# Seven Strassen quarter products for the eight of a down projection, in a one-layer streaming encoder step

## Chip, cores and metric

The kernel runs on one core of a Trainium2 chip, in one launch. The metric is the device time in microseconds (us). The kernel before took 2740.11 us as the median of three runs (2739.68, 2740.11 and 2749.0).

## The reference

One step of a one-layer encoder in float32, for 2048 prompt tokens and 64 sample tokens of width 1024. The mixer (a gated linear recurrence with four heads, and a gated recurrent unit with a short convolution) stands ahead of the part that changes; six modulation vectors come from a matrix `w_ada` for the prompt and for the sample each.

```python
mod = jax.nn.silu(c) @ w_ada + b_ada
sh1, sc1, g1, sh2, sc2, g2 = jnp.split(mod[:, None, :], N_MOD, axis=-1)
hn = _rms(x) * (1 + sc1) + sh1
...
x = x + g1 * y
hn2 = _rms(x) * (1 + sc2) + sh2
x = x + g2 * (jnp.square(jax.nn.relu(hn2 @ w_up)) @ w_down)
...
y = _rms(x) * final_gain
```

`w_up` is 1024 x 4096, `w_down` 4096 x 1024. The change is to the product with `w_down`.

## The kernel before, in words

The prompt is worked on in four blocks of 512 tokens; the last block carries the 64 sample tokens too. A block goes through phase A (first norm and its transpose, `XT`), the projections and mixers, phase O (output projection, residual, second norm), and the MLP. Every float32 product is made of three matmuls of split operands (`HL`): high by high, high by low, low by high. `split_raw` (L245) makes both parts of a weight unit of 128x1024: ScalarE casts the high part (L247), and VectorE or GpSimd subtracts it for the low part (L248). `CFG` says which engine: of the up units each second one went to GpSimd, the down units to VectorE.

The MLP goes over eight groups of 512 columns. `phase_U` (U) of a group is 96 matmuls of 128x512 (L901) into the PSUM pool `pmu`; ScalarE takes relu (L904) and its square as the high part (L906), VectorE squares again (L907) and subtracts for the low part (L908), into a tile `gt` of the pool `mgp` (two buffers). `phase_D` (D) is 96 matmuls (L942; 112 in the last block, with the sample) into `pmd`, two buffers, one PSUM tile for each 128 tokens and 512 output columns; VectorE adds each to its row of `acc` in SBUF (L946; ScalarE copies in the first group). The last group, D7, multiplies by the gate (L948), adds (L949) to what phase F0 has made of `acc` on GpSimd (L965, L966), and ends with the final norm (phase F).

The program writes U0, U1, D0, U2, D1 and so on, U7, phase A of the next block, D6, D7. `sec` gives each part a rank from which the scheduler makes the order of every engine's queue. SyncE issues all loads. Within blocks 0 to 2, from the second group on, some sums of the sample's modulation vectors stand between (`ada_s`, run 5 times a block): VectorE takes a loaded tile of `w_ada` times one entry of silu(c) for each partition and adds it up, in 256 columns at a time (`ada_first`, L271, L273) or 1024 (`ada_part`, L308, L310); one tiny matmul for each 128 columns (L280, L314) sums over partitions. These loads used the pool `vop`, five buffers.

## Time and profile before

| | us |
|---|---|
| median of three runs | 2740.11 |
| span of the profiled execution | 2745.4 |
| TensorE busy (L901 745.3, L942 754.2) | 2554.4 |
| VectorE busy | 1635.4 |
| ScalarE busy | 946.6 |
| GpSimd busy | 481.7 |
| weight splits L248 on VectorE (253) / GpSimd (131) | 314.9 / 319.1 |

The profiled execution's span is 5.3 us above the median of the runs. Its granted TensorE clock was 0.965 of the full 2.4 GHz over the span. Busy time is the time in which an engine has an instruction under way; an instruction that waits inside the engine for a port counts as busy, so an operation's duration can hold a wait. "Releaser" in a row, behind `<-`, is the instruction whose end let the next one start.

### The profile page before, as it was taken

Reading aid. Unit: us, or ns where it says so; the run is one execution under the profiler, and the core shown is the slowest. Engines: PE = TensorE matmul, PEld = TensorE weight load, DVE = VectorE, ACT = ScalarE, POOL = GpSimd, SP = SyncE. Lnnn points to the kernel's source line nnn. Section 1 sums busy time; section 2 is a strip of 40 time slices with the busy share of each in tenths; the row PEclk is TensorE's granted clock in tenths of the full one; section 3 lists DMA queues with packets and bytes.
Section 4 is the critical chain, followed back from the end, with each engine's and each line's share of the span. In section 5 each row is a group of like instructions: output and inputs, shape, how many; then the busy total and the mean of one; then the engine's idle time right before and its main releaser. Section 6 shows DMA issues by size and latency. Waiting matters only on the chain.

```text
span 2745.4 us, 35118 instructions
## 1 busy us (share of the span) xinstructions
PE 2554.4 (93%) x13868; PEld 2180.5 (79%) x13868; DVE 1635.4 (60%) x3007; ACT 946.6 (34%) x1511; POOL 481.7 (18%) x292
## 2 busy tenths in 40 slices
PE   5898999999988999999898999999898899999996
PEld 4876887887866788888776788888798788988995
DVE  6678745566466765554746874544736677344446
ACT  4353442223325353223325253222322625422321
POOL 2311111011322110100323111010323211011003
PEclk8998999999999999999999999999999999999998
DMA  6242434444411335444511233423432233222222
GB/s 235 93 158 80 169 130 139 142 149 161 138 47 62 115 110 168 135 135 145 175 55 62 85 126 113 153 89 104 158 108 62 32 101 109 92 81 77 88 89 74
DMA packets 93477, 311.75 MB, mean 114 GB/s; under 512 B 15072, under 2 KB 17024, under 8 KB 92288
## 3 DMA queue, kind: packets, MB, share of 16 engines
q1 hardware_dynamic: 93312, 309.50, 34.0%
q8 instruction: 109, 1.79, 0.3%
q14 instruction: 56, 0.46, 0.0%
HBM read 291.60 MB, written 17.86 MB: 113 GB/s over the span
## 4 chain that ended last, share of the span: by engine, by line
PE 73%; DVE 18%; issue 3%; ACT 3%; DMA 2%; POOL 1%; SPq 0%; DVEq 0%; ACTq 0%; POOLq 0%
PE ps_u L901 26%; PE ps_d L942 20%; PE ps_in L584 7%; PE ps_vo L695 6%; PE ps_y L867 4%; PE ps_lv L770 3%; DVE hd_h L774 2%; DVE rsp L350 1%; DVE wt L248 1%; PE ps_in L569 1%; DVE hd_h L775 1%; PE ps_rg L644 1%; DVE rgtmp L640 1%; DMA x_a<-in_x_prompt_dram 1%; DVE acc L949 1%
## 5 line engine op out<-in xcount | busy, mean ns | idle before, releaser
L942 PE MATMUL ps_d<-wt,gt 128*128 128x512 f32 x3200 | 754.2, 396 | 32.6 <-DVE hd_f L948 14.8
L901 PE MATMUL ps_u<-XT,wt 128*128 128x512 f32 (+2 forms) x4128 | 745.3, 341 | 13.7 <-DVE XT L377 9.2
L942 PEld LDWEIGHTS ps_d<-wt,gt 128*128 128x128 f32 x3200 | 605.4, 191 | 172.8 <-DVE acc L946 19.5
L901 PEld LDWEIGHTS ps_u<-XT,wt 128*128 128x128 f32 x4128 | 656.6, 190 | 95.1 <-DVE XT L377 10.8
L247 ACT CAST wt<-raw 128x1024 fp32r<-128x1024 f32 x384 | 400.0, 1046 | 500.8 <-PE ps_d L942 386.7
L248 POOL TENSOR_TENSOR wt<-raw,wt 128x1024 fp32r<-128x1024 f32 x131 | 319.1, 2443 | 1274.1 <-ACT wt L247 1253.9
L248 DVE TENSOR_TENSOR wt<-raw,wt 128x1024 fp32r<-128x1024 f32 x253 | 314.9, 1246 | 370.5 <-ACT wt L247 370.3
L584 PE MATMUL ps_in<-XT,wt 128*128 128x512 f32 (+1 forms) x1776 | 392.9, 370 | 7.0 <-POOL wt L248 3.9
L584 PEld LDWEIGHTS ps_in<-XT,wt 128*128 128x128 f32 x1776 | 296.7, 195 | 50.8 <-issue 5.0
L904 ACT ACTIVATE hd_u<-ps_u 128x512 f32<-128x512 f32 (+2 forms) x172 | 85.6, 498 | 463.0 <-PE ps_u L901 462.9
L946 DVE TENSOR_TENSOR acc<-acc,ps_d 128x512 f32<-128x512 f32 x204 | 138.7, 682 | 153.7 <-PE ps_d L942 153.6
L695 PE MATMUL ps_vo<-wt,XT 128*128 128x256 f32 x1600 | 205.6, 288 | 7.7 <-ACT vo L704 6.0
L695 PEld LDWEIGHTS ps_vo<-wt,XT 128*128 128x128 f32 x1600 | 199.4, 195 | 9.9 <-ACT vo L704 5.9
L907 DVE TENSOR_TENSOR hd_u<-hd_u 128x512 f32<-128x512 f32 (+2 forms) x172 | 148.3, 862 | 97.9 <-ACT gt L906 97.8
L867 PE MATMUL ps_y<-wt,mix 128*128 128x512 f32 x800 | 195.7, 399 | 0.6 <-DVE rst L346 0.3
L867 PEld LDWEIGHTS ps_y<-wt,mix 128*128 128x128 f32 x800 | 149.1, 190 | 32.5 <-DVE rst L346 0.7
L770 PEld LDWEIGHTS ps_lv<-hd_h 128*128 128x128 f32 x640 | 92.8, 218 | 48.8 <-issue 33.7
L770 PE MATMUL ps_lv<-hd_h 128*128 128x64 f32 x640 | 95.3, 298 | 36.2 <-DVE hd_h L775 35.0
L774 DVE TENSOR_TENSOR hd_h<-hd_h 128x256 f32<-128x256 f32 x112 | 79.8, 712 | 51.5 <-PE ps_lv L770 40.4
L310 DVE SCALAR_TENSOR_TENSOR ada_acc<-raw,silc,ada_acc 128x1024 f32<-128x1024 f32 x56 | 76.3, 1363 | 39.9 <-DMA raw<-in_w_ada_dram 39.5
L908 DVE TENSOR_TENSOR gt<-hd_u,gt 128x512 fp32r<-128x512 f32 (+2 forms) x172 | 97.0, 564 | 4.7
L906 ACT ACTIVATE gt<-hd_u 128x512 fp32r<-128x512 f32 (+2 forms) x172 | 91.3, 533 | 1.3
(261 smaller groups left out, 1981.6 us busy)
## 6 DMA issues: line engine op xcount, KB each, us to landing
raw<-in_w_up_dram SPq DMA_DIRECT2D x128, 512.0 KB, 3.6
raw<-in_w_down_dram SPq DMA_DIRECT2D x128, 512.0 KB, 3.5
raw<-in_w_in_dram SPq DMA_DIRECT2D x96, 512.0 KB, 3.5
raw<-in_w_ada_dram SPq DMA_DIRECT2D x80, 512.0 KB, 3.6
raw<-in_w_out_dram SPq DMA_DIRECT2D x32, 512.0 KB, 3.5
x_a<-in_x_prompt_dram SPq DMA_DIRECT2D x16, 512.0 KB, 4.5
x<-in_x_prompt_dram SPq DMA_DIRECT2D x16, 512.0 KB, 5.2
x2d<-x SPq DMA_DIRECT2D x16, 512.0 KB, 3.0
```

The source lines that it names most:

```text
L247: S.copy(wt[:, 0], raw)
L248: eng.tensor_tensor(wt[:, 1], raw, wt[:, 0].bitcast(F32), op=ALU.subtract)
L584: T.matmul(ps[:, :pn], lhsT=w[:, a, k], rhs=B.XT.p[x][:, k, p0:p0 + pn], start=(k == 0 and q == 0), stop=(k == KD - 1 and q == 2))
L695: T.matmul(ps[:rows(B.toks[ti]), :256], lhsT=l, rhs=ws[k // 4][:, a, k % 4], start=(q == 0), stop=(q == len(ops) - 1))
L770: T.matmul(ps[:C, c * C // 2:(c + 1) * C // 2].rearrange("p (b h) -> p b h", h=hs), lhsT=KS[:, c * C:c * C + C], rhs=qv[:, c * bc:(c + 1) ...
L774: V.tensor_tensor(qv[:, :, 1], qv[:, :, 1], tv[:, :, 0:1].to_broadcast([P, nb, hs]), op=ALU.mult)
L867: T.matmul(ps[:rows(B.toks[ti])], lhsT=l, rhs=ws[k - k % 2][:, a, k % 2], start=(q == 0), stop=(q == len(ops) - 1))
L901: T.matmul(ps[:, :pn], lhsT=w[:, a, k], rhs=B.XT.p[x][:, k, p0:p0 + pn], start=(k == 0 and q == 0), stop=(k == KD - 1 and q == 2))
L907: V.tensor_mul(r, r, r)
L908: B.ulast = V.tensor_tensor(gt.p[1][:, c, p0:p0 + pn], r, gh.bitcast(F32), op=ALU.subtract)
L942: T.matmul(ps[:nr], lhsT=l, rhs=ws[half][c // 2][:, a, c % 2], start=(q == 0), stop=(q == len(ops) - 1))
L946: V.tensor_tensor(ac[:nr, sl], ac[:nr, sl], ps[:nr], op=ALU.add)
```

## The change

Of the eight groups' D, the first seven become W (`phase_W`): the product of the group's activations (512 tokens x 512) with its weights (512 x 1024) is cut into quarters and formed from seven products of quarters in place of eight (Strassen's scheme in Winograd's form). A product is two token tiles of six matmuls: 84 for a W, where D had 96; the sample's tokens get 16 of their own as before. The products M1, M6 and M7 are accumulated over the seven groups in tiles of their own (`accM`), the others in the quarters of `acc`; `combine` adds them up once a block, ahead of D7. `down_units` makes the seven weight operands, `sums_of` the seven of the activations, in two tiles `gX` and `gY` that take both buffers of `mgp`. The product order is A11, A12, S1, S4, S2, S3, A22, their PSUM tiles by turns in `pmd` (two buffers) and `pax` (three).

```diff
-CFG = dict(hd=2, w=6, raw=3, gr='G', f0='GGGGG', blk=32, proj='GG', proj0='GV', vo0='GG', vo='VV', up='VG', down='VV')
+CFG = dict(hd=2, w=5, raw=5, gr='G', f0='GGGGG', blk=32, proj='GG', proj0='GV', vo0='GG', vo='VV', up='VV', down='VV')
...
-    vop = pool("vop", 5)
+    vop = pool("vop", 7)
...
+    def ada_raw(src):
+
+        raw = rowp.tile([P, 1028], F32, tag="row", name="raw")[:, :1024]
...
+        def split(n, raw):
+            hi, lo = op[n]
+            S.copy(hi, raw)
+            return V.tensor_tensor(lo, raw, hi.bitcast(F32), op=ALU.subtract)
+
+        split("A11", A11)
+        split("A12", A12)
+        split("A22", A22)
+        V.tensor_tensor(A22, A21, A22, op=ALU.add)
+        split("S1", A22)
+        V.tensor_tensor(A21, A11, A21, op=ALU.subtract)
+        V.tensor_tensor(A11, A22, A11, op=ALU.subtract)
+        V.tensor_tensor(A12, A12, A11, op=ALU.subtract)
+        split("S4", A12)
+        split("S2", A11)
+        B.ulast = split("S3", A21)
...
+    def down_units(g):
...
+        w11, w21 = split(r11), split(r21)
+        E.tensor_tensor(r11, r12, r11, op=ALU.subtract)
+        t1 = split(r11)
+        w22 = split(r22)
+        E.tensor_tensor(r11, r22, r11, op=ALU.subtract)
+        t2 = split(r11)
+        E.tensor_tensor(r12, r22, r12, op=ALU.subtract)
+        t3 = split(r12)
+        E.tensor_tensor(r21, r21, r11, op=ALU.subtract)
+        t4 = split(r21)
...
+        M1, M6, M7 = (B.accM[n] for n in (1, 6, 7))
+        lo, hi = slice(0, 512), slice(512, 1024)
+        for t in range(2):
+            add(G, B.acc[t][:, lo], M1[:, t])
+        add(V, M6, M1)
+        for t in range(2):
+            add(V, B.acc[t][:, hi], M6[:, t])
+        for t in range(2):
+            add(V, B.acc[t][:, hi], B.acc[2 + t][:, hi])
+        add(G, M7, M6)
+        for t in range(2):
+            av = B.acc[2 + t].rearrange("p (h c) -> p h c", h=2)
+            add(G, av, M7[:, t].unsqueeze(1).to_broadcast([P, 2, 512]))
...
+            if g:
+                with sec(b, 115 + 10 * g):
+                    (phase_D if g == NG else phase_W)(B, g - 1, gts[g - 1])
             if g == NG - 1 and not B.last:
                 with sec(b, 182):
                     phase_A(blocks[b + 1], B.ulast)
             if g:
-                with sec(b, 115 + 10 * g):
-                    phase_D(B, g - 1, gts[g - 1])
```

`E` in `down_units` is GpSimd; VectorE's own square is left out for the first seven groups, and `hd` goes from ScalarE's square straight to `sums_of`. The up splits all go to VectorE. The loads of `w_ada` for the sample go through `rowp`, two buffers. The gate matrices `rgw` and the sample's state are loaded once a block into `vop`, the gate matrices laid out on the host; the sample's low parts are no longer copied a second time for `gt` and `mix`. The last line of the diff writes the next block's phase A behind W6 instead of ahead of D6; it is still gated on U7's last split.

The order of the engines' queues moves in three places.

**First place.** VectorE in the MLP of block 0, where the sample's first modulation vectors are summed. Before (L271, L273, L277: the modulation sums; L907, L908: U's square and low part; L946: the evacuation):

```order
L907 TENSOR_TENSOR hd_u<-hd_u 128x512
L273 SCALAR_TENSOR_TENSOR ada_acc<-raw,silc,ada_acc 128x256
L908 TENSOR_TENSOR gt<-hd_u,gt 128x512
L273 SCALAR_TENSOR_TENSOR ada_acc<-raw,silc,ada_acc 128x256 x3
L277 TENSOR_TENSOR ada_acc<-ada_acc 128x256
L907 TENSOR_TENSOR hd_u<-hd_u 128x512
L946 TENSOR_TENSOR acc<-acc,ps_d 128x512
L908 TENSOR_TENSOR gt<-hd_u,gt 128x512
L271 TENSOR_SCALAR ada_acc<-raw,silc 128x256
L273 SCALAR_TENSOR_TENSOR ada_acc<-raw,silc,ada_acc 128x256
L946 TENSOR_TENSOR acc<-acc,ps_d 128x512 x2
```

Now (L268, L270, L282: the same sums; L938: the split of an activation operand; L1042: the evacuation of W):

```order
L938 TENSOR_TENSOR gX<-hd_u,gX 128x512
L286 TENSOR_TENSOR modc<-ps_ada,cols 128x2
L270 SCALAR_TENSOR_TENSOR ada_acc<-raw,silc,ada_acc 128x256 x2
L282 TENSOR_TENSOR ada_acc<-ada_acc 128x256
L268 TENSOR_SCALAR ada_acc<-raw,silc 128x256 x2
L270 SCALAR_TENSOR_TENSOR ada_acc<-raw,silc,ada_acc 128x256 x6
L282 TENSOR_TENSOR ada_acc<-ada_acc 128x256
L268 TENSOR_SCALAR ada_acc<-raw,silc 128x256
L270 SCALAR_TENSOR_TENSOR ada_acc<-raw,silc,ada_acc 128x256 x3
L1042 TENSOR_TENSOR accM<-accM,ps_d 128x512 x2
L1042 TENSOR_TENSOR acc<-acc,ps_d 128x512 x4
```

The sums stood between squares and evacuations; now they stand in one block behind the last split of the activation sums and ahead of the group's first evacuation.

**Second place.** GpSimd over one group of block 0. Before, the 16 operations of the eight groups' up units stood in one row, two of them a group:

```order
L248 TENSOR_TENSOR wt<-raw,wt 128x1024 x16
```

Now one group is (L1011: the split of a weight operand; L1015, L1020, L1018, L1022: the weight sums):

```order
L1015 TENSOR_TENSOR raw<-raw 128x1024
L1020 TENSOR_TENSOR raw<-raw 128x1024
L1011 TENSOR_TENSOR wt<-raw,wt 128x1024 x2
L1018 TENSOR_TENSOR raw<-raw 128x1024
L1022 TENSOR_TENSOR raw<-raw 128x1024
L1011 TENSOR_TENSOR wt<-raw,wt 128x1024 x5
```

Eleven operations of 128x1024 stand where two stood (the last of the five splits in the bottom row is the first of the next group).

**Third place.** VectorE behind the fourth product's evacuation of W6, at the end of a block (L1071: the combination; L245: weight splits of D7 and, the last, of the next block; L1111: D7's first results; L489: the next block's norm):

```order
L1042 TENSOR_TENSOR accM<-accM,ps_d 128x512 x4
L1042 TENSOR_TENSOR acc<-acc,ps_d 128x512
L1071 TENSOR_TENSOR accM<-accM 128x1024
L1042 TENSOR_TENSOR acc<-acc,ps_d 128x512
L1071 TENSOR_TENSOR acc<-acc,accM 128x512 x2
L1071 TENSOR_TENSOR acc<-acc 128x512 x2
L245 TENSOR_TENSOR wt<-raw,wt 128x1024 x3
L1111 TENSOR_TENSOR hd_f<-ps_d,row 128x512
L245 TENSOR_TENSOR wt<-raw,wt 128x1024
L489 TENSOR_SCALAR ss_a<-ss_a 128x4
```

and GpSimd in the same place (L1128, L1129: phase F0):

```order
L1011 TENSOR_TENSOR wt<-raw,wt 128x1024 x3
L1071 TENSOR_TENSOR acc<-acc,accM 128x512 x2
L1011 TENSOR_TENSOR wt<-raw,wt 128x1024
L1071 TENSOR_TENSOR accM<-accM 128x1024
L1071 TENSOR_TENSOR acc<-acc,accM 128x1024 x2
L1128 TENSOR_TENSOR acc<-acc,row 128x1024 x4
L1129 TENSOR_TENSOR acc<-acc,x2r 128x1024 x4
```

Ten operations of the combination have come in ahead of D7 and of phase F0; three weight splits of D7 stand behind VectorE's part of them.

## Rows read from the trace of the kernel before

**Rows 1.** The page's head and part 1: busy time, share, count by engine.

```profile
span 2745.4 us, 35118 instructions
...
PE 2554.4 (93%) x13868; PEld 2180.5 (79%) x13868; DVE 1635.4 (60%) x3007; ACT 946.6 (34%) x1511; POOL 481.7 (18%) x292
```

**Rows 2.** The page, part 4: the chain that ended last, by engine.

```profile
PE 73%; DVE 18%; issue 3%; ACT 3%; DMA 2%; POOL 1%; SPq 0%; DVEq 0%; ACTq 0%; POOLq 0%
```

**Rows 3.** Windows (busy PE, PEld, DVE, ACT, POOL; PEclk; DMA): with, without modulation work.

```profile
1083.11:1128.44 45.33, 45.33 (x210) 37.66 (x208) 21.67 (x26) 13.51 (x17) 4.79 (x2) 1.00 0.33 105
1816.94:1860.81 43.87, 43.87 (x196) 36.06 (x195) 18.09 (x24) 11.41 (x15) 4.98 (x3) 1.00 0.30 96
```

**Rows 4.** Timeline of TensorE: one U, the D behind it (block 1).

```profile
1037.52 21.92 PE L901 MATMUL ps_u<-XT,wt 128*128 128x512 f32 x96
1059.28 5.60 PE L942 MATMUL ps_d<-wt,gt 128*128 128x512 f32 x24
```

**Rows 5.** The page, part 5: the weight split on GpSimd and VectorE.

```profile
L248 POOL TENSOR_TENSOR wt<-raw,wt 128x1024 fp32r<-128x1024 f32 x131 | 319.1, 2443 | 1274.1 <-ACT wt L247 1253.9
L248 DVE TENSOR_TENSOR wt<-raw,wt 128x1024 fp32r<-128x1024 f32 x253 | 314.9, 1246 | 370.5 <-ACT wt L247 370.3
```

**Rows 6.** By line (ns min/median/max): modulation step L310, evacuation L946.

```profile
L310 DVE SCALAR_TENSOR_TENSOR ada_acc<-raw,silc,ada_acc x56: 1271/1284/2558, 130.1 to 1763.2; 128x1024 f32<-128x1024 f32 x56
...
L946 DVE TENSOR_TENSOR acc<-acc,ps_d x204: 671/680/689, 423.5 to 2693.4; 128x512 f32<-128x512 f32 x102
```

**Rows 7.** Timeline of VectorE, 1100 to 1116 us (block 1).

```profile
1102.34 0.68 DVE L907 TENSOR_TENSOR hd_u<-hd_u 128x512 f32<-128x512 f32 x1
1103.06 0.69 DVE L908 TENSOR_TENSOR gt<-hd_u,gt 128x512 fp32r<-128x512 f32 x1
1107.16 2.46 DVE L907 TENSOR_TENSOR hd_u<-hd_u 128x512 f32<-128x512 f32 x1 [3.42 <-ACT gt L906]
```

**Rows 8.** Timeline of GpSimd, the same stretch.

```profile
1106.68 2.40 POOL L248 TENSOR_TENSOR wt<-raw,wt 128x1024 fp32r<-128x1024 f32 x1 [30.88 <-ACT wt L247]
```

**Rows 9.** Timeline of GpSimd, 609 to 616 us (block 0).

```profile
611.30 3.16 POOL L248 TENSOR_TENSOR wt<-raw,wt 128x1024 fp32r<-128x1024 f32 x1 [8.19 <-ACT wt L247]
```

**Rows 10.** Timeline of VectorE, the same stretch.

```profile
610.20 0.35 DVE L271 TENSOR_SCALAR ada_acc<-raw,silc 128x256 f32<-128x256 f32 x1 [2.13 <-DMA raw<-in_w_ada_dram]
610.59 0.49 DVE L273 SCALAR_TENSOR_TENSOR ada_acc<-raw,silc,ada_acc 128x256 f32<-128x256 f32 x1
610.99 1.22 DVE L248 TENSOR_TENSOR wt<-raw,wt 128x1024 fp32r<-128x1024 f32 x1
```

**Rows 11.** Timeline of GpSimd, phase F0 at the end of block 3.

```profile
2703.07 5.59 POOL L965 TENSOR_TENSOR acc<-acc,row 128x1024 f32<-128x1024 f32 x2 [11.90 <-DVE rsq L351]
2708.63 4.71 POOL L966 TENSOR_TENSOR acc<-acc,x2r 128x1024 f32<-128x1024 f32 x2
```

**Rows 12.** Timeline of VectorE, the same stretch.

```profile
2711.03 5.63 DVE L949 TENSOR_TENSOR acc<-acc,hd_f 128x512 f32<-128x512 f32 x2 [3.39 <-POOL acc L966]
...
2719.58 2.14 DVE L949 TENSOR_TENSOR acc<-acc,hd_f 128x512 f32<-128x512 f32 x1
```

**Rows 13.** The page, part 6: modulation loads, last column issue to landing.

```profile
raw<-in_w_ada_dram SPq DMA_DIRECT2D x80, 512.0 KB, 3.6
```

**Rows 14.** Windows: boundary behind block 0, a stretch inside it.

```profile
643.82:704.68 60.86, 52.35 (x222) 42.32 (x220) 44.99 (x70) 22.62 (x39) 19.85 (x8) 0.92 0.49 175
...
666.00:672.00 6.00, 5.01 (x16) 4.36 (x17) 3.56 (x10) 1.68 (x3) 2.36 (x1) 0.50 0.17 66
```

**Rows 15.** Timeline of TensorE at that boundary.

```profile
666.99 2.05 PE L470 MATMUL ps_rs<-ident,rsq 128*128 128x128 f32 x8 [3.77 <-DVE rsq L351]
...
693.58 4.42 PE L942 MATMUL ps_d<-wt,gt 128*128 128x512 f32 x12 [2.99 <-DVE hd_f L948]
```

**Rows 16.** Tile x_a: loads; VectorE timeline: last write of XT.

```profile
L449 SPq DMA_DIRECT2D x_a<-in_x_prompt_dram x12: 327/328/579, 648.6 to 1943.2; - x12
...
685.33 0.73 DVE L481 SCALAR_TENSOR_TENSOR XT<-x_a,modc,XT 128x512 fp32r<-128x512 f32 x1
```

More of the change, by code (lines that the diff above doesn't have):

```diff
@@ L97, in layout @@
     xt = a["x_prompt"][0].reshape(-1, BLK, 4, 2, P)
+    gate_w = np.zeros((P, 4, 2, P), np.float32)
+    for m, nm in enumerate(("rg_wa", "rg_wx")):
+        for c in range(4):
+            for hf in range(2):
+                sl = slice(hf * 64, hf * 64 + 64)
+                gate_w[sl, c, m, sl] = a[nm][0][2 * c + hf]
+    d["rg_w"] = gate_w.reshape(P, D)
     d["x_t"] = np.ascontiguousarray(xt.transpose(0, 2, 4, 3, 1)).reshape(-1, 4, P, 2 * BLK)
@@ L811, in hg_chunks @@
             if g.which:
-                dst = Sst_s[:, h]
+                dst = B.Ss[:, h]
             else:
@@ L904, in phase_U @@
             S.activation(r, ps[:, :pn], AF.Relu)
+            if not plain:
+                S.activation(r, r, AF.Square)
+                continue
             gh = gt.p[0][:, c, p0:p0 + pn]
@@ new lines, in phase_W, with evac @@
+    def phase_W(B, g, op):
+        if g == 0:
+            B.acc = [vop.tile([P, D], F32, tag="vo", name="acc") for _ in range(4)]
+            B.accM = {n: vop.tile([P, 2, 512], F32, tag="vo", name="accM") for n in (1, 6, 7)}
+            if B.last:
+                B.acc.append(adp.tile([P, D], F32, tag="ada", name="acc_s"))
+        ws = down_units(g)
+        M = {n: [B.accM[n][:, t] for t in range(2)] for n in (1, 6, 7)}
+        for n, ti, half in ((2, 0, 0), (3, 0, 1), (4, 2, 0), (5, 2, 1)):
+            M[n] = [B.acc[ti + t][:, half * 512:half * 512 + 512] for t in range(2)]
+        def evac(dst, ps):
+            if g == 0:
+                return S.copy(dst, ps)
+            return V.tensor_tensor(dst, dst, ps, op=ALU.add)
+        pools = ((pmd, "md"), (pax, "ax"))
+        for q, (n, x, wi) in enumerate(((1, "A11", 0), (2, "A12", 1), (5, "S1", 2), (3, "S4", 3), (6, "S2", 4),
+                                        (7, "S3", 5), (4, "A22", 6))):
+            pool_, tag = pools[q % 2]
+            w = ws[wi]
+            for t in range(2):
+                ps = pool_.tile([P, 512], F32, tag=tag, name="ps_d")
+                ops = [(c, y, a) for c in range(2) for a, y in HL]
+                for k, (c, y, a) in enumerate(ops):
+                    T.matmul(ps, lhsT=op[x][y][:, c, t * P:(t + 1) * P], rhs=w[:, a, c],
+                             start=(k == 0), stop=(k == len(ops) - 1))
+                last = evac(M[n][t], ps)
+                if g == 0 and q == 0:
+                    acc0[:] = [last]
+            if B.last and wi in (0, 1, 3, 5):
+                half, form = {0: (0, 0), 1: (0, 1), 3: (1, 2), 5: (1, 3)}[wi]
+                if form % 2 == 0:
+                    ps_s = pmu.tile([P, 512], F32, tag="mu", name="ps_s")
+                for k in range(4):
+                    T.matmul(ps_s, lhsT=op["s"][:, form, k // 2], rhs=w[:, k % 2, k // 2],
+                             start=(form % 2 == 0 and k == 0), stop=(form % 2 == 1 and k == 3))
+                if form % 2:
+                    evac(B.acc[4][:, half * 512:half * 512 + 512], ps_s)
@@ L929, in phase_D @@
+    def phase_D(B, g, gt):
+        rows2 = {}
+        if B.last:
+            rows2[1] = row_load(gscr[3], LS, B.ulast)
+        fg = row_load(i["final_gain"], P, B.ulast)
+        rows2[0] = row_load(gscr[2], P, B.ulast)
+        combine(B)
+        ws = {}
+        for ti, half in [(ti, half) for ti in B.order for half in range(2)]:
             if half not in ws:
@@ L933, in phase_D @@
             ac = B.acc[ti]
-            if lastg and half == 0:
+            if half == 0:
                 ss = smp.tile([P, 8], F32, tag="ss", name="ss_f")
```

151 lines of the change are left out of this document (95 added, 56 removed).

## Prediction, written before the changed kernel ran

> **What bounds the kernel now.** I read the page's totals first, then its chain of waits, then the timelines of the stages that the change touches. TensorE is busy 2554.4 of 2745.4 us, and 13,868 of its instructions follow each other with little between; VectorE is busy 60%, GpSimd 18% [rows 1]. The chain that ended last lies 73% on TensorE and 18% on VectorE [rows 2]. So fewer matmuls save time only where TensorE is what ends last, and the quarter that is not TensorE's shows where VectorE already holds it up. Inside the MLP it does not: a period of one U and one D without modulation work is 43.87 us with TensorE busy 43.87, and with modulation work 45.33 of 45.33 [rows 3]. The profiled execution's span is 5.3 us above the median of the runs, 2740.11; I make the sum on the span and take 5.3 off at the end.
>
> **What is removed.** 96 matmuls of U(g) last from 1037.52 to the start of D at 1059.28, 21.76 us, so a matmul of 128x512 costs 0.2267 us [rows 4]. A Strassen product takes 7 x 2 x 6 = 84 matmuls where D took 96; the sample keeps 16. Twelve fewer in 7 groups of 4 blocks: 28 x 12 x 0.2267 = **76.2 us off**. This is all that the change can gain.
>
> **What is added.** GpSimd splits all seven weight operands and makes the four weight sums, 11 operations a group, where it had two (the second place of the order, above). One splits in 2.44 us, on VectorE in 1.25 [rows 5]: 11 x 2.40 = 26.4 us of a period that is to last 43.9 - 2.7 = 41.1 us. By its own load it fits. VectorE does all four up splits now (4 x 1.25 = 5.0 us), 11 two-input operations on activations of 0.69 and 14 evacuations of 0.68 [rows 5 to 7]: 5.0 + 7.6 + 9.5 = 22 us of 41. That fits too. ScalarE gets three casts more a group; it is 34% busy [rows 1]. The small edits (the gate matrices and the sample's state loaded once a block, no copies of the sample's low parts) I take at nothing: they stand beside the projections, and the DMA engines are busy 0.30 to 0.33 in the MLP [rows 3]; without that cover one load would cost its 3.6 us to landing [rows 13].
>
> **What the loads don't say.** The square of the activations, two SBUF inputs on VectorE, takes 0.68 us at 1102.34 and 2.46 at 1107.16 [rows 7]. GpSimd's split stands from 1106.68 to 1109.08 [rows 8]; the long one starts after it and ends 0.5 us behind its end. An evacuation, which has one input in PSUM, never took more than 0.689 us in 204 [rows 6]. So a VectorE operation with two SBUF inputs waits until a GpSimd operation in progress is over. It holds the other way too: a GpSimd split that met a VectorE one lasted 3.16 us [rows 9, 10]. Where GpSimd runs back to back, VectorE gets one such operation for each of GpSimd's: at 2711 two adds of 128x512 took 5.63 us, one at 2719.58 took 2.14, beside GpSimd's adds of 128x1024 at 4.71 and 5.59 us a pair [rows 11, 12]. The modulation's 128x1024 operation stretches the same way, from 1.28 to 2.56 us [rows 6].
>
> The Trainium skill has the rule in "GPSIMD Engine Reference", section "Specifications", the row on SBUF interfaces: GpSimd shares them with VectorE and contends with VectorE instructions that have two SBUF inputs or use a two-port mode. The trace agrees (0.68 against 2.46 us). It speaks against this change: by engine loads alone the time would be 2664 us, by the rule it is the sum below.
>
> **A group without modulation work.** Let t = 0 be the start of U(g). TensorE needs the first evacuation of W(g-1) at 21.8 + 24 x 0.2267 = 27.2, because A11 and A12 fill four PSUM buffers and S1 needs one of the first two back. VectorE makes the sums until about 14, one for one with GpSimd's first three operations and waiting for ScalarE's copies between. GpSimd's other eight splits and sums then run from about 15 to 36 (8 x 2.40 plus some 0.2 each for meeting VectorE); the products want the last four at 30, 33, 36 and 38. That is in time by 3 to 4 us: no cost taken, and 0.75 us in each of 20 such groups, 15 us, as the upper end.
>
> **Groups with the sample's modulation sums.** Before, these operations stand singly between the others; now they stand in one block after the sums and ahead of the first evacuation (the first place of the order). Their inputs come through two buffers, where five were shared before, and one load takes 3.6 us to land [rows 13]. In block 0 three groups have 22, 16 and 25 such operations of 0.35 to 0.49 us [rows 10]. Eight of them go beside GpSimd's eight, until 36; the rest take 0.45 each: 36 + 14 x 0.45 = 42, 39.6 and 43.6. The first evacuation is wanted at 27.2, so TensorE stands 15, 12 and 16 us. In block 1 groups with seven, seven and five of the 1.28 us operations, and in block 2 one with seven, go at 3.4 us each (2.40 and the 1.0 that VectorE's turn adds): 14 + 6 x 3.4 + 1.3 = 35.7, 8.5 us late three times, and 2 once. After TensorE had stood 3.8 us its granted clock was 0.50 for the six us that followed [rows 14], so half of 6 us is lost behind each of six long stalls, 18 us. Sum: 43 + 27.5 + 18 = **88 us**. The lower end is 0: at their own durations 22 x 0.48 or 8 x 1.28 us after 14 end by 24.6, ahead of 27.2. I take the upper one, since it is the row in which GpSimd runs without gaps that is nearest.
>
> **Block boundaries.** From D6's start to D7's end it was 60.9 us, 8.5 of them with TensorE idle [rows 14]; it waited 3.77 for the next block's norm and up to 2.99 at once for D7's results to be taken [rows 15]. Now (the third place of the order) the combination of the seven products goes ahead of D7: four operations of 0.69 us and one of 1.25 on VectorE, five on GpSimd, and GpSimd's eight of phase F0 behind them. The last three weight splits of D7 stand behind these on VectorE and take GpSimd's 2.4 each rather than 1.2. W6 ends 19 us after its start; 4 to 13 us later D7 has its first weights, where it had them before. I take 7, and 5 more between its halves. The next block's first norm is gated on U7's last split, which waits for a buffer that W6 frees after its fourth product; its loads, on SyncE's queue, begin about 19 us after W6's start, where they began at 4.8 (643.82 to 648.6), so its XT comes at some 60 where it came at 42 [rows 16]. That takes the next block's value matmuls, which filled TensorE's gaps there, out of reach. Net of these some 11 us for each of three boundaries, **33 us**; bounds 0 (all hidden behind F0, which was there before) and 16. At the end of the last block there is no next norm: 4 us.
>
> **The sum.** 2745.4 - 76.2 + 88 + 33 + 4 = 2794; less 5.3, **2789 us**, 1.8% slower. With every upper bound (15 for the plain groups, 48 for the boundaries, 5 more at the end) it is 2824.
>
> **Rivals.**
> - *The saving stays.* The operations of VectorE find gaps on GpSimd, as GpSimd waits for casts, loads and its five weight buffers, and TensorE's queue keeps its 96 matmuls of U as cover. For it: GpSimd's idle time before a split was almost always ScalarE's cast [rows 5], so it ran one operation at a time and left gaps. Against: it then had two operations a group. All stalls 0, boundaries as they were: 2664; with a third of the stalls 2705. Chance 0.2. It decides if the first evacuation stands ahead of 28 in the groups with modulation work.
> - *Stalls and saving cancel.* Half of the modulation stalls and two thirds of the boundaries: 2745.4 - 76.2 + 44 + 22 + 4 - 5.3 = 2734. Within 0.5% (2726 to 2754, about what a measurement of this kernel can tell from no change): chance 0.13.
> - *GpSimd becomes the bound everywhere.* If GpSimd pays the 0.95 us of [rows 9] for each of the four up splits and 0.4 for the other eleven, its 11 operations take 34.6 us, and with buffers of weights freed late the last weight is late in all 28 groups by some 2 us and their clock is disturbed: 2789 + 56 = 2845. Chance 0.1, within slower.
> - *It doesn't do what it says.* The matmul count is fixed in the program: 12 fewer a group are there. No chance taken.
>
> **How the numbers follow.** The forecast, stalls in the modulation groups and at the boundaries, has 0.57; the third rival 0.1; together slower 0.67, same 0.13, faster 0.2. The range: low 2712, which leaves the first rival's full form out (0.13), high 2845, which leaves about 0.07 above.
>
> **What would show it.** In the changed profile: VectorE's 256-column modulation operations at 2 us or more where GpSimd is busy; TensorE idle 10 us or more in a single place in three groups of block 0 and three later ones, the releaser a VectorE evacuation, with the granted clock at 0.50 (1.2 GHz) behind; plain groups at 41 us. I am wrong if the modulation groups have a period of 43 us or less (first rival), or if plain groups last over 43 (third).

## The result, and the profile after

The changed kernel took 2842.67 us, the median of four runs (2839.93 to 2847.38); the kernel before took 2741.83 in four runs beside it (2739.68 to 2749.0). The ratio is 1.037, with an interval of 1.035 to 1.039: 3.7% slower, where 1.8% slower was forecast. The profiled run's span is 92.8 us above that of before.

The page of the changed kernel: its head, part 1 (beside [rows 1]), and from part 5 the weight splits on GpSimd and VectorE (beside [rows 5]).

```profile
span 2838.2 us, 35269 instructions
...
PE 2510.9 (88%) x13532; PEld 2135.5 (75%) x13532; DVE 2008.1 (71%) x3131; ACT 1152.7 (41%) x1836; POOL 1196.1 (42%) x540
...
L1011 POOL TENSOR_TENSOR wt<-raw,wt 128x1024 fp32r<-128x1024 f32 x196 | 507.7, 2610 | 581.9 <-ACT wt L1010 530.9
...
L245 DVE TENSOR_TENSOR wt<-raw,wt 128x1024 fp32r<-128x1024 f32 x205 | 287.2, 1405 | 110.0 <-ACT wt L244 108.1
```

TensorE has its 336 matmuls less, and now stands idle for 12% of the span. VectorE and GpSimd are not full: 71% and 42%. By these shares neither of the two bounds the kernel, so the stages have to be read. Windows of the changed kernel, with the columns of [rows 3] (the last is GB/s): a group of block 0 with modulation work, two stretches inside it, a plain group, and the four block ends from W6's start to D7's end, the last to the end of the span.

```profile
485.55:542.82 57.27, 42.94 (x186) 34.88 (x186) 51.19 (x54) 19.31 (x26) 26.44 (x11) 0.88 0.31 110
505.00:525.00 20.00, 7.85 (x35) 6.17 (x33) 16.85 (x17) 4.16 (x5) 12.39 (x6) 0.77 0.35 122
525.00:531.00 6.00, 5.19 (x15) 4.16 (x16) 3.62 (x7) 0.48 (x1) 0.00 (x0) 0.63 0.50 203
1844.83:1885.80 40.97, 40.97 (x182) 33.71 (x181) 27.28 (x27) 19.48 (x26) 26.88 (x11) 1.00 0.27 96
679.97:764.09 84.12, 59.31 (x225) 46.15 (x224) 69.94 (x99) 29.07 (x47) 45.58 (x18) 0.82 0.43 150
1341.95:1425.78 83.83, 59.31 (x231) 46.31 (x229) 68.79 (x94) 28.35 (x45) 47.32 (x19) 0.84 0.43 151
1993.02:2083.66 90.64, 60.23 (x234) 47.77 (x232) 72.14 (x113) 32.20 (x54) 49.55 (x21) 0.81 0.42 145
2743.32:2838.20 94.88, 57.43 (x214) 43.36 (x212) 76.48 (x133) 19.62 (x39) 46.55 (x19) 0.81 0.24 75
```

The plain group is what the change promised: 40.97 us, TensorE busy throughout, GpSimd's eleven operations (26.88 us) hidden. The modulation group, 58.31 us from its U's start at 483.71 to the next U's at 542.02 (the window above is 1 us shorter), stands 17 us above it, and behind its stall the clock is 0.63 for six us. The block end that took 60.86 us [rows 14] takes 84.12: TensorE is idle for 24.8 us of it where it was for 8.5, and 225 matmuls keep it busy for 59.31 us where 222 took 52.35, at a clock of 0.82 for 0.92.

To see where 92.8 us come from, I cut both spans at the first matmul of each block's U0 and of its D6 or W6:

| us | start to U0 | U0 to D6/W6, blocks 0, 1, 2, 3 | D6/W6 to the next U0, blocks 0, 1, 2, and to the end |
|---|---|---|---|
| before | 321.9 | 321.9, 321.7, 319.0, 367.4 | 321.4, 320.3, 374.1, 77.7 |
| after | 325.4 | 354.5, 321.6, 310.5, 345.3 | 340.4, 340.6, 405.0, 94.9 |

Inside the blocks six shorter groups should take off 16.3 each. Blocks 0 to 2 are 48.9, 16.2 and 7.8 above that, and block 3, which has no modulation work, 5.8 below. From W6 on, where 10.9 should come off, 87.4 have come on. (The last column holds the next block's norm, projections and mixers too, whose matmuls fill gaps beside D7.)

TensorE's timeline in block 0 of the changed kernel, beside [rows 4], and the longest waits in blocks 1 and 2:

```profile
507.25 5.60 PE L1053 MATMUL ps_d<-wt,gX 128*128 128x512 f32 x24
525.81 7.41 PE L1053 MATMUL ps_d<-wt,gX 128*128 128x512 f32 x24 [12.96 <-DVE accM L1042]
...
581.78 8.38 PE L1053 MATMUL ps_d<-wt,gX 128*128 128x512 f32 x24 [12.30 <-DVE accM L1042]
...
615.69 1.01 PE L285 MATMUL ps_ada<-ones,ada_acc 128*128 128x1 f32 x4 [7.41 <-DVE ada_acc L282]
...
641.99 7.32 PE L1053 MATMUL ps_d<-wt,gX 128*128 128x512 f32 x24 [4.64 <-DVE accM L1042]
...
1167.39 7.46 PE L1053 MATMUL ps_d<-wt,gX 128*128 128x512 f32 x24 [9.09 <-DVE accM L1042]
...
1218.78 7.36 PE L1053 MATMUL ps_d<-wt,gX 128*128 128x512 f32 x24 [6.63 <-DVE accM L1042]
...
1829.15 7.68 PE L1053 MATMUL ps_d<-wt,gX 128*128 128x512 f32 x24 [7.35 <-DVE accM L1042]
```

The four filled PSUM tiles are there at 512.85; the first evacuation comes at 524.99. VectorE in that time:

```profile
507.98 2.51 DVE L282 TENSOR_TENSOR ada_acc<-ada_acc 128x256 f32<-128x256 f32 x1
510.42 4.85 DVE L268 TENSOR_SCALAR ada_acc<-raw,silc 128x256 f32<-128x256 f32 x2
515.19 4.53 DVE L270 SCALAR_TENSOR_TENSOR ada_acc<-raw,silc,ada_acc 128x256 f32<-128x256 f32 x6
...
521.30 0.35 DVE L268 TENSOR_SCALAR ada_acc<-raw,silc 128x256 f32<-128x256 f32 x1 [1.12 <-DMA raw<-in_w_ada_dram]
...
524.06 1.00 DVE L270 SCALAR_TENSOR_TENSOR ada_acc<-raw,silc,ada_acc 128x256 f32<-128x256 f32 x2 [1.89 <-DMA raw<-in_w_ada_dram]
524.99 1.28 DVE L1042 TENSOR_TENSOR accM<-accM,ps_d 128x512 f32<-128x512 f32 x2
```

and GpSimd:

```profile
507.62 9.84 POOL L1011 TENSOR_TENSOR wt<-raw,wt 128x1024 fp32r<-128x1024 f32 x4
```

While GpSimd runs its four splits back to back, VectorE gets one operation done for each of them, 2.4 to 2.5 us apiece; the moment GpSimd is through, at 517.46, VectorE is back at its own pace. An operation of 128x256 costs here what GpSimd's operation of 128x1024 costs. Of the stall's last 7.5 us, behind GpSimd's end, 3.0 are two waits of VectorE for modulation loads.

The block end behind block 1 on TensorE, beside [rows 15] (L1110: D7; L493: the next block's norm):

```profile
1363.14 5.46 PE L1053 MATMUL ps_d<-wt,gY 128*128 128x512 f32 x12 [4.71 <-DVE accM L1042]
...
1376.07 2.08 PE L1110 MATMUL ps_d<-wt,gt 128*128 128x512 f32 x4 [4.89 <-DVE wt L245]
...
1392.35 2.08 PE L493 MATMUL ps_rs<-ident,rsq 128*128 128x128 f32 x8 [2.77 <-DVE rsq L356]
...
1407.29 11.34 PE L1110 MATMUL ps_d<-wt,gt 128*128 128x512 f32 x36 [4.85 <-DVE hd_f L1111]
1422.06 3.01 PE L1110 MATMUL ps_d<-wt,gt 128*128 128x512 f32 x12 [3.42 <-DVE hd_f L1111]
```

GpSimd there, the combination (L1071) and phase F0 (L1128, L1129):

```profile
1372.28 5.96 POOL L1071 TENSOR_TENSOR acc<-acc,accM 128x1024 f32<-128x1024 f32 x2 [1.90 <-DVE acc L1071]
1378.20 12.29 POOL L1128 TENSOR_TENSOR acc<-acc,row 128x1024 f32<-128x1024 f32 x4
1408.48 2.37 POOL L1129 TENSOR_TENSOR acc<-acc,x2r 128x1024 f32<-128x1024 f32 x1 [17.99 <-DMA x2r<-x2d]
```

and VectorE beside it:

```profile
1372.66 9.96 DVE L245 TENSOR_TENSOR wt<-raw,wt 128x1024 fp32r<-128x1024 f32 x3
...
1385.88 2.32 DVE L489 TENSOR_SCALAR ss_a<-ss_a 128x4 f32<-128x4 f32 x1
```

Three splits of D7 take 9.96 us, where alone they would take 3.7. Nothing of this end is one long wait: the five shown are of 2.8 to 4.9 us, each behind another step of one row of work. At the last end one wait is longer, for a weight split of D7:

```profile
2782.01 2.08 PE L1110 MATMUL ps_d<-wt,gt 128*128 128x512 f32 x4 [10.16 <-DVE wt L245]
```

GpSimd's wait of 17.99 us is no collision: the loads for F0's second half go through the two buffers of the next block's norm, and that norm is late.

### The profile page after: what moved, and what is told of

Read it like the earlier page. It is cut to its first block, busy times and chain, and to the rows that moved or that the text cites. A ratio compares the mean times of both kernels' runs of the same rounds, so it can differ in the third digit from the quotient of the medians.

```text
span 2838.2 us, 35269 instructions
## 1 busy us (share of the span) xinstructions
PE 2510.9 (88%) x13532; PEld 2135.5 (75%) x13532; DVE 2008.1 (71%) x3131; ACT 1152.7 (41%) x1836; POOL 1196.1 (42%) x540
## 5 line engine op out<-in xcount | busy, mean ns | idle before, releaser
L1011 POOL TENSOR_TENSOR wt<-raw,wt 128x1024 fp32r<-128x1024 f32 x196 | 507.7, 2610 | 581.9 <-ACT wt L1010 530.9
L244 ACT CAST wt<-raw 128x1024 fp32r<-128x1024 f32 x271 | 281.0, 1048 | 272.7 <-PE ps_d L1053 130.1
L1053 PE MATMUL ps_d<-wt,gX 128*128 128x512 f32 x1344 | 325.2, 400 | 56.1 <-DVE accM L1042 54.3
L245 DVE TENSOR_TENSOR wt<-raw,wt 128x1024 fp32r<-128x1024 f32 x205 | 287.2, 1405 | 110.0 <-ACT wt L244 108.1
L1053 PEld LDWEIGHTS ps_d<-wt,gX 128*128 128x128 f32 x1344 | 259.5, 194 | 114.1 <-issue 55.3
L245 POOL TENSOR_TENSOR wt<-raw,wt 128x1024 fp32r<-128x1024 f32 x66 | 162.0, 2468 | 276.5 <-ACT wt L244 276.5
L1053 PE MATMUL ps_d<-wt,gY 128*128 128x512 f32 x1008 | 242.6, 397 | 16.1 <-DVE accM L1042 14.7
L1053 PEld LDWEIGHTS ps_d<-wt,gY 128*128 128x128 f32 x1008 | 192.2, 192 | 60.7 <-issue 16.4
L1010 ACT CAST wt<-raw 128x1024 fp32r<-128x1024 f32 x196 | 204.8, 1045 | 78.8 <-PE ps_d L1053 40.5
L1042 DVE TENSOR_TENSOR accM<-accM,ps_d 128x512 f32<-128x512 f32 x144 | 94.3, 679 | 152.4 <-PE ps_d L1053 152.4
L1110 PE MATMUL ps_d<-wt,gt 128*128 128x512 f32 x400 | 128.8, 484 | 79.1 <-DVE hd_f L1111 42.8
L1042 DVE TENSOR_TENSOR acc<-acc,ps_d 128x512 f32<-128x512 f32 x192 | 128.3, 683 | 72.3 <-PE ps_d L1053 71.8
L1110 PEld LDWEIGHTS ps_d<-wt,gt 128*128 128x128 f32 x400 | 93.1, 241 | 111.9 <-DVE hd_f L1111 47.7
```

The costliest lines, as they stand in the source:

```text
L244: S.copy(wt[:, 0], raw)
L245: eng.tensor_tensor(wt[:, 1], raw, wt[:, 0].bitcast(F32), op=ALU.subtract)
L1010: S.copy(t[:, 0], r)
L1011: E.tensor_tensor(t[:, 1], r, t[:, 0].bitcast(F32), op=ALU.subtract)
L1042: return V.tensor_tensor(dst, dst, ps, op=ALU.add)
L1053: T.matmul(ps, lhsT=op[x][y][:, c, t * P:(t + 1) * P], rhs=w[:, a, c], start=(k == 0), stop=(k == len(ops) - 1))
```

## The experiments

Two theories stood. By the first, GpSimd's two-input operations and VectorE's, one at a time through a shared interface, make both losses. By the second, order and buffers do: the block of modulation sums ahead of the evacuations, the two load buffers, the late gate of the norm. Times of the kernel before beside these runs were 2742.5, 2746.0, 2745.0, 2746.5 and 2743.3 us; a kernel without an interval was run once. The four runs of the changed kernel lie within 7.5 us, and e12 and e17, one kernel, have 2725.26 and 2728.46 to 2732.91, so a step of under 8 us between single runs settles nothing. The three stages, each of the profiled run, cut as above and summed over the four blocks, are these:

| us | time | start | U0 to D6/W6 | D6/W6 to U0 or end |
|---|---|---|---|---|
| before | 2741.83 | 321.9 | 1329.9 | 1093.5 |
| after | 2842.67 | 325.4 | 1331.9 | 1180.9 |
| e1_no_sample_mod | 2754.96 | 328.8 | 1240.5 | 1183.9 |
| e2_one_input_gpsimd | 2748.28 | 328.9 | 1248.4 | 1169.3 |
| e4_four_splits_vector | 2796.67 | 327.9 | 1296.8 | 1170.1 |
| e8_seven_splits_vector | 2767.32 | 329.1 | 1266.6 | 1168.2 |
| e3_norm_gate | 2853.73 | 329.5 | 1333.6 | 1188.8 |
| e5_combine_vector | 2829.11 | 328.6 | 1331.8 | 1166.9 |
| e6_f0_vector | 2824.56 | 328.2 | 1331.9 | 1162.6 |
| e7_x2_other_buffers | 2851.29 | 329.1 | 1331.4 | 1189.0 |
| e9_splits_combine_f0 | 2742.18 | 327.4 | 1266.0 | 1147.0 |
| e10_and_norm_gate | 2732.24 | 328.9 | 1268.0 | 1133.6 |
| e11_and_late_u7_split | 2737.50 | 330.7 | 1268.3 | 1136.7 |
| e12_and_d7_splits_gpsimd | 2725.26 | 328.3 | 1265.5 | 1129.7 |
| e13_gpsimd_d7_no_late_split | 2728.96 | 329.2 | 1267.0 | 1130.5 |
| e14_mod_spread | 2735.57 | 328.6 | 1264.8 | 1139.8 |
| e15_norm_behind_d7 | 2748.41 | 327.6 | 1266.7 | 1151.1 |
| e16_spread_and_norm_behind | 2741.27 | 327.1 | 1261.7 | 1150.7 |
| e17_best_five_rounds | 2728.69 | 327.1 | 1267.0 | 1137.0 |
| e18_before_f0_vector | 2705.25 | 319.8 | 1331.0 | 1055.4 |

**The modulation groups.** e1 leaves the sample's modulation sums out.

```diff
-    ada_s = [ada_part(G2, 0), ada_first(1)] + [ada_part(p, 1) for p in range(2, 6)]
+    ada_s = [ada_part(G2, 0)]
+    V.memset(modc[:, :, 1], 0.0)
```

> Edit: the changed kernel without the sample's modulation vectors (they are set to zero; the prompt's second gate is still summed). Theory 'stalls in the modulation groups': the waits of TensorE for VectorE's first evacuation in six groups of blocks 0 to 2 (12.96, 12.30, 12.05, 9.09, 6.63 and 7.35 us in the changed kernel, with the slow clock behind them some 85 us) go, and some 1.5 us of TensorE's own sums in 11 groups with them: 2842 falls to about 2740, and every group has a period of 41 us. Rival 'GpSimd is the bound in every group': no more than 25 us go.

Measured 2754.96: 87.7 off, all of it inside the blocks (1331.9 to 1240.5), while the block ends stayed. That sizes the loss but doesn't say why: the sums are gone, and with them both theories' cause. e2 keeps every instruction in its place and takes GpSimd's second input away (the weights' low parts and sums are wrong for it).

```diff
-            E.tensor_tensor(t[:, 1], r, t[:, 0].bitcast(F32), op=ALU.subtract)
+            E.tensor_scalar(t[:, 1], t[:, 0].bitcast(F32), 1.0, None, op0=ALU.mult)
...
-        E.tensor_tensor(r11, r12, r11, op=ALU.subtract)
+        E.tensor_scalar(r11, r12, 1.0, None, op0=ALU.mult)
```

> Edit: the eleven GpSimd operations of a group read one tensor in place of two (the weights' low parts and sums are wrong for it), same size, same place in the queue, same waits for ScalarE. Theory 'the port': a VectorE operation waits for a GpSimd one of two SBUF inputs; without a second input the modulation operations take their 0.45 us or 1.28 us and the stalls go: about 2842 - 85 = 2755, and less at the boundaries. Rival 'the order': the block of modulation operations ahead of the first evacuation, fed by two buffers at 3.6 us a load, is late by itself: 2830 or more, the six waits of 7 to 13 us stay. Either way the run tells what one GpSimd operation of one input takes, and whether it blocks.

Measured 2748.28. GpSimd of e2 in the group that stood 12.96 us before, and the page's row for its splits:

```profile
484.32 6.61 POOL L1015 TENSOR_SCALAR raw<-raw 128x1024 f32<-128x1024 f32 x1
491.02 2.95 POOL L1020 TENSOR_SCALAR raw<-raw 128x1024 f32<-128x1024 f32 x1
```

```profile
L1011 POOL TENSOR_SCALAR wt<-wt 128x1024 fp32r<-128x1024 f32 x196 | 557.3, 2859 | 421.5 <-ACT wt L1010 385.1
```

and VectorE beside it:

```profile
489.67 3.24 DVE L270 SCALAR_TENSOR_TENSOR ada_acc<-raw,silc,ada_acc 128x256 f32<-128x256 f32 x6
```

GpSimd is busy for longer than before (2859 ns a split for 2610, 1273.6 us in all), and still six of VectorE's sums pass in 3.24 us where three operations took 7.4. The block of sums and its two load buffers are the same, and VectorE still waits for loads in it, 1.48 us at most in this group. So it is the pair of two-input operations, not GpSimd's load, not the order and not the buffers; the second theory falls for these groups. All sums of this kind (L270), in the changed kernel and in e2 (ns, min/median/max):

```profile
L270 DVE SCALAR_TENSOR_TENSOR ada_acc<-raw,silc,ada_acc x48: 468/485/2699, 496.9 to 671.8; 128x256 f32<-128x256 f32 x48
...
L270 DVE SCALAR_TENSOR_TENSOR ada_acc<-raw,silc,ada_acc x48: 468/476/1257, 489.7 to 620.7; 128x256 f32<-128x256 f32 x48
```

Against e2, blocks 0 to 2 of the changed kernel are 82 us longer inside (1331.9 less 1248.4, without block 3's 1.5).

e4 and e8 keep the work and move four, then all seven, of a group's weight splits to VectorE, where each takes half as long:

```diff
-        w11, w21 = split(r11), split(r21)
+        w11, w21 = split(r11, V), split(r21, V)
...
-        t1 = split(r11)
-        w22 = split(r22)
+        t1 = split(r11, V)
+        w22 = split(r22, V)
```

> Edit: four of the seven weight splits of a group (t1, w22, t2, t3) go to VectorE, GpSimd keeps seven operations. Theory 'the port': what both engines want of it in a group falls from 11 x 2.40 + 12.6 = 39 us to 7 x 2.40 + 4 x 1.25 + 12.6 = 34.4 us; the six stalls get shorter by a third to a half, 30 to 45 us in all: 2800 to 2812. Rival 'the order': VectorE only has more in its queue ahead of the evacuations: 2842 or more.

> Edit: all seven weight splits of a group go to VectorE, GpSimd keeps the four weight sums. Theory 'the port': wanted in a group 4 x 2.40 + 7 x 1.25 + 12.6 = 31 us where it was 39; the six stalls behind modulation operations nearly go, at 2842 - 65 = 2777 or less; four splits gave 46. Rival 'VectorE's queue': VectorE's own work is 31 us of 41 and 39 in the modulation groups, its evacuations come late behind splits, and it is 2797 (as with four) or more.

Measured 2796.67 and 2767.32. Inside the blocks e8 takes 1266.6 us; before less 24 groups of 2.72 is 1264.6. As much as the whole saving is there, with VectorE carrying more work.

**The block ends, one part at a time.** e3 opens the next norm's gate at U7's relu, in place of its last split:

```diff
-                    phase_A(blocks[b + 1], B.ulast)
+                    phase_A(blocks[b + 1], B.urelu)
```

> Edit: the next block's first norm is gated on ScalarE's last relu of U7 in place of VectorE's last split of U7. Theory 'the late norm ends the boundary': D7 ends 17 us behind the last piece of XT, because its last operand (x2) comes through the same two buffers as the norm's rows; the norm's loads start some 10 to 15 us earlier, and each of three boundaries (84.1, 83.0, 90.6 us from W6's start) gets 10 to 15 us shorter: about 2842 - 38 = 2805. Rival 'the combination and D7's weight splits end it': under 8 us in all, 2835 or more.

Measured 2853.73, 11 slower than the changed kernel and 6 above the slowest of its runs; 8 of the 11 lie at the block ends. The norm did come earlier, and then stood against F0. VectorE of e3 behind block 0, and GpSimd:

```profile
721.55 6.68 DVE L502 SCALAR_TENSOR_TENSOR x_a<-x_a,modc,hd_a 128x512 f32<-128x512 f32 x3 [1.03 <-ACT hd_a L495]
728.16 8.34 DVE L504 SCALAR_TENSOR_TENSOR XT<-x_a,modc,XT 128x512 fp32r<-128x512 f32 x3
```

```profile
724.88 11.06 POOL L1128 TENSOR_TENSOR acc<-acc,row 128x1024 f32<-128x1024 f32 x4
```

The norm's operations that take 2.08 us for three, alone, take 6.68 and 8.34. The late gate alone was not the cause; it had kept two colliding parts apart. e7 gave F0's loads other buffers (`rawp` for `xap`), e5 put the combination and e6 phase F0 on VectorE.

```diff
-        add(G, M7, M6)
+        add(V, M7, M6)
...
-CFG = dict(hd=2, w=5, raw=5, gr='G', f0='GGGGG', blk=32, proj='GG', proj0='GV', vo0='GG', vo='VV', up='VV', down='VV')
+CFG = dict(hd=2, w=5, raw=5, gr='G', f0='VVVVV', blk=32, proj='GG', proj0='GV', vo0='GG', vo='VV', up='VV', down='VV')
...
-        x2 = xap.tile([P, D], F32, tag="xa", name="x2r")
+        x2 = rawp.tile([P, 1024], F32, tag="raw", name="x2r")
```

> Edit: the five GpSimd operations of the combination (two of 128x512, three of 128x1024) go to VectorE. Now read: at the boundary behind block 1 they hold GpSimd and the port for 11 to 12 us, and phase F0 stands behind them. Theory 'the boundary is one chain through the port: combination, F0's first half, norm, F0's second half': the five take 2 x 0.69 + 3 x 1.25 = 5.1 us, everything behind them comes 5 to 6 us earlier, at all four block ends: 2842 - 22 = 2820. Rival 'the three weight splits of D7, which stand behind it on VectorE, set D7': VectorE's queue gets longer, 2842 to 2850.

> Edit: phase F0's eight operations of 128x1024 in a block go from GpSimd to VectorE (1.25 us each in place of 2.5). Theory 'one chain through the port': F0 takes 10 us in place of 20 and no longer stands one for one against the norm's operations; 6 to 10 us less at each of four block ends: 2805 to 2818. Rival 'F0 is not on the path': 2835 or more.

> Edit: F0's second operand (x2, loaded back) comes through the weight buffers in place of the two that the next block's norm uses. Theory 'D7 ends 17 us behind the norm because x2 waits for the norm's buffers' (18 us of GpSimd's waits behind block 1 are for that load): D7 ends 8 to 12 us earlier at three boundaries, nothing at the last: 2842 - 30 = 2812. Rival 'the port chain alone sets D7's end, the buffers are incidental': under 8 us, 2835 or more.

Measured 2829.11, 2824.56 and 2851.29: 13.6 and 18.1 off, less than expected, and 8.6 on. In e7 three of the four operations of F0's second half no longer waited for loads and stood against the norm instead, whose first matmul waited 16.83 us:

```profile
735.99 2.08 PE L493 MATMUL ps_rs<-ident,rsq 128*128 128x128 f32 x8 [16.83 <-DVE rsq L356]
```

At the ends behind blocks 0 and 1 neither e5 nor e6 took off more than 4 us; e5's gain lies behind block 2 (10.5 us) and e6's at the end (11.0). That the next step of the row is late each time too would explain it, and was not followed up.

**All together, and the order behind it.** e9 is e8, e5 and e6 in one. e10 adds e3's gate. e11 adds to e10 a later rank for U7's square and split, among W6's evacuations, and opens D7's late loads at ScalarE's relu; e12 is e11 with D7's weight splits on GpSimd, which is free there now.

```diff
+            with sec(B.b, 186.5):
-            V.tensor_mul(r, r, r)
+                V.tensor_mul(r, r, r)
...
-CFG = dict(hd=2, w=5, raw=5, gr='G', f0='VVVVV', blk=32, proj='GG', proj0='GV', vo0='GG', vo='VV', up='VV', down='VV')
+CFG = dict(hd=2, w=5, raw=5, gr='G', f0='VVVVV', blk=32, proj='GG', proj0='GV', vo0='GG', vo='VV', up='VV', down='GG')
```

> Edit: the three that gained, together: seven splits, the combination and phase F0 on VectorE; GpSimd keeps the weight sums and the mixers' work. Theory 'two places, one port': the gains lie in different stages (75 us in the modulation groups, 14 and 18 at the block ends) and add: 2842 - 107 = 2735, a little under the kernel before. Rival 'at the block end they were two roads to the same gain': 2749 or more.

> Edit: the run before, and the next norm gated on ScalarE's last relu of U7. By itself that cost 11 us, with the norm one for one against F0 on GpSimd. Theory 'the port': with nothing of two inputs left on GpSimd at the block end, the earlier norm gains what it should have, 5 to 10 us at each of three boundaries: 2735 - 22 = 2713. Rival 'VectorE's order': the norm stands ahead of D7's weight splits on VectorE and D7 waits for these, as with the gate alone: 2735 or more.

> Edit: as the run before, with U7's last squares and splits on VectorE behind W6's evacuations (they stood ahead of four of them and held TensorE 3.5 to 4.7 us before W6's last product), and the late loads of D7 gated on ScalarE's relu too. Theory: 3 us at each of four block ends, 10 us under the run before. Rival: D7 then waits for that split, no change.

> Edit: as the run before, with D7's four weight splits on GpSimd, which has nothing else there. Theory 'D7's splits stand behind the combination and the norm on VectorE' (TensorE waits 5 to 10 us for them at each block end): 5 us or more at each of four ends, 20 us under the run before. Rival 'the port': four times 2.40 us of GpSimd against a VectorE full of two-input operations cost what they give: within 5 us, or slower.

e9 took 2742.18: the three gains nearly add (100.5 of 75.4 + 13.6 + 18.1 = 107). These moves took 66 us off inside the blocks and 34 at the ends. At the ends that is not the collision alone: the combination and F0 are also half as long on VectorE (1.22 us for 2.4), and no run there does what e2 does in the groups, keeping GpSimd's load without its second input. e10 took 2732.24: the gate that made the block ends 8 us longer in e3 makes them 13 shorter here, with F0 off GpSimd (10 in all, where 22 were expected); the change of sign is what the first theory asks for. e11 took 2737.50, 5 more than e10 where less was expected: a miss. e12 took 2725.26, 12 less than e11, where 20 were expected, and 7 less than e10, which the spread does not settle. VectorE of e12 behind block 0, where D7's splits on GpSimd (8.29 us for three) meet U7's late square and split:

```profile
660.82 0.68 DVE L1044 TENSOR_TENSOR accM<-accM,ps_d 128x512 f32<-128x512 f32 x1
661.42 2.29 DVE L995 TENSOR_TENSOR hd_u<-hd_u 128x512 f32<-128x512 f32 x1
663.63 2.83 DVE L998 TENSOR_TENSOR gt<-hd_u,gt 128x512 fp32r<-128x512 f32 x1
```

e13 to e16 try to keep e12's gain without this. e13 is e10 with D7's splits on GpSimd; e14 spreads the modulation sums over six groups for five; e15 ranks the next norm behind D7 on VectorE; e16 is e14 and e15 in one.

```diff
-                    if 1 < g < 7 and not B.last:
-                        run(ada_s, -(-64 // (5 * (NB - 1))))
+                    if 1 < g < 8 and not B.last:
+                        run(ada_s, -(-64 // (6 * (NB - 1))))
...
-                with sec(b, 182):
+                with sec(b, 196):
```

> Edit: splits, combination and F0 on VectorE, the norm gated on ScalarE's relu, D7's weight splits on GpSimd; U7's own split stands where it stood. In the run with all five edits D7 waited 7 to 8 us for U7's late split, behind GpSimd's three splits of D7. Theory 'late split is a loss': 4 to 6 us at each of four block ends come back, less the 2.4 to 4.7 that W6's last product waits again: 2725 - 10 = 2715. Rival: they balance, 2722 to 2728.

> Edit: as the run before, with the sample's modulation sums spread over six groups of a block, four loads each, where it was five groups and five loads. Theory 'what is left of the stalls in the modulation groups is a matter of how many stand ahead of the first evacuation': the 2 to 4.5 us left in four groups go, 8 to 12 us under the run before. Rival: the same, or more stalls in more groups.

> Edit: as the first of these runs, with the next block's norm ranked behind D7 on VectorE. With the norm ahead, D7's first evacuation waits 5 to 10 us behind it. Theory 'VectorE's order at the block end decides': D7 runs earlier, but XT comes later and with it the matmuls that fill the gaps: within 6 us of the first of these runs. Rival 'the norm ahead is the loss': 10 us or more under it.

> Edit: the two runs before together. If their effects lie in different stages they add, within 3 us.

Measured 2728.96, 2735.57, 2748.41 and 2741.27: none beats e12. e13 and e14 went with their rivals (e13 lies 1 us above its range), e15 with neither, and the effects of e14 and e15 don't add in e16. e15 shows what an order that the change left alone is worth: phase A has rank 182 in both kernels, ahead of D7, and behind D7 it costs 19 us.

**Price of the best version, and of F0 alone.** e17 is e12 again. e18 is the kernel before, with one word changed and no Strassen product:

```diff
-CFG = dict(hd=2, w=6, raw=3, gr='G', f0='GGGGG', blk=32, proj='GG', proj0='GV', vo0='GG', vo='VV', up='VG', down='VV')
+CFG = dict(hd=2, w=6, raw=3, gr='G', f0='VVVVV', blk=32, proj='GG', proj0='GV', vo0='GG', vo='VV', up='VG', down='VV')
```

> The kernel of e12 (seven splits, combination and F0 on VectorE; norm and D7's loads gated on ScalarE's relu; U7's split behind W6's evacuations; D7's weight splits on GpSimd), timed in five rounds. One look gave 2725.3 beside 2745.0: a ratio of 0.993. Theory: the gain over the kernel before is real and small, 0.5 to 0.8%. Rival: it is within the spread of single looks, 0.997 or more.

> Edit to the kernel before: phase F0 on VectorE, no Strassen product. It tells whether the repair of the block ends would have paid without the product. Theory 'F0 was no bound there': the kernel before had GpSimd idle at its block ends but for F0, and its norm ran beside it; within 6 us of the kernel before. Rival 'the same port cost was in the kernel before': 10 us or more under it.

e17: 2728.69 (six runs), ratio 0.994 (0.993 to 0.996) to the kernel before, 2743.31 beside it (eleven runs). e18: 2705.25 (four runs, 2696.74 to 2713.64), ratio 0.985 (0.983 to 0.988). Page and windows of e18, the first and the last block end, and TensorE's wait for the norm:

```profile
PE 2537.0 (94%) x13868; PEld 2169.5 (80%) x13868; DVE 1630.1 (60%) x3041; ACT 948.4 (35%) x1511; POOL 394.7 (15%) x258
```

```profile
641.73:694.62 52.89, 51.47 (x254) 43.23 (x253) 42.97 (x82) 24.12 (x40) 0.00 (x0) 1.00 0.57 193
2636.04:2706.20 70.16, 53.25 (x226) 42.78 (x224) 50.18 (x113) 13.05 (x28) 0.24 (x1) 0.90 0.27 87
```

```profile
664.91 1.13 PE L470 MATMUL ps_rs<-ident,rsq 128*128 128x128 f32 x8 [1.26 <-DVE rsq L351]
```

The block ends of [rows 14] and [rows 15] had the collision before the change too: TensorE's wait of 3.77 us for the norm falls to 1.26, the end from 60.86 to 52.89 us with more matmuls in it, the clock there from 0.92 to 1.00. I had expected no difference. VectorE took on 34 operations of 1.22 us, 41 us, and is busy for 5 us less than before, so its others are 47 us shorter: they no longer wait. F0's own time falls too, by some 9 us a block (eight operations at 1.22 for 2.4), and how much of the gain is that and how much the collision was not parted. e18 beats both kernels, and e12.

## Why the prediction was right in direction and too small by half

*The saving and the plain groups* were right. Plain groups last 40.97 us for a forecast of 41, and e8 has inside the blocks all that 24 groups can save.

*The modulation groups* were right in cause and, against e2, in size: 82 us for a forecast of 88. The stalls of block 0 were 12.96, 12.30 and 7.41 + 4.64 for 15, 12 and 16, with the releaser as forecast but for the 7.41 (a sum, L282), and a slow clock behind the first, 0.63 over six us for 0.50. Those of blocks 1 and 2 were 9.09, 6.63 and 7.35 for 8.5 each. So two of the six, not all, reached the 10 us in one place that the forecast named as its sign. Against the kernel before, blocks 0 to 2 lost 72.9, 15 below the forecast, since before was itself not free of the loss (1329.9 less the saving is 16 above e2).

*The step that failed* is the block boundaries, "net of these some 11 us for each of three boundaries", 33 us, with bounds of 0 and 16 each, and "at the end of the last block there is no next norm: 4 us". Together 37; from W6 on, the four ends measured 87.4 + 10.9 = 98 us, 20 to 34 each. Four faults lie in that one term. I priced the combination, D7's splits and the norm by their own lateness and let each lie beside the others, though I had said that VectorE gets one operation for each of GpSimd's: then they follow each other. Behind block 1 TensorE waits for W6's own evacuation (4.71 us, nothing in the sum), D7's weights (4.89), the norm (2.77) and twice for D7's results to be taken (4.85 and 3.42, for "5 more between its halves"). I gave these waits no slow clock, though I had charged one in the modulation groups: of the 23 us by which the end behind block 0 grew, 16 are idle time and 7 slower matmuls. I took the last end as nearly free because the norm is missing there, while combination, F0 and D7 alone make 20 us, 10.16 of them in one wait for D7's weights. And I set the lower bound, 0, by "hidden behind F0, which was there before"; F0 was no free cover: moved off GpSimd in the kernel before, it gave 38 us of block ends back (e18).

What the runs say of the 98: 34 went with GpSimd's operations (e9), and 13 more with the earlier gate of the norm once these are gone (e10). D7's splits and U7's late split took off 4 more in e12, but e17, the same kernel, has 7 more than e12 there, so that is not settled. Some 50 stay open. In e9 VectorE alone carries the combination, D7's splits, F0 and the norm in one queue; which order of these would be shortest was not found.

*The sum.* 2794 was forecast for the span, 2838.2 came: 61 from the ends, less 15 in the modulation groups, less 6 in block 3, whose groups went from 51.53 to 48.13 us, 3.4 for the 2.72 of 12 matmuls, and 3.5 more at the start, a stage that none of these edits touches and that took 327 to 331 in the experiments on the changed kernel (neither was followed up). The remaining 10 us to the median come from the two profiled runs: the span of before lay 5.3 above the median, this one 4.5 below.

*The rivals.* "The saving stays" failed at its own test: in the first of the modulation groups the first evacuation came 41 us after U's start, for 28. "Stalls and saving cancel" asked for 2726 to 2754. "GpSimd becomes the bound everywhere" named 2845, close to the time, but by a mechanism that didn't occur: the plain groups lose nothing. (Its 0.95 us of [rows 9] is 0.76 against the 2.40 of [rows 8]; little hangs on it.)
